# Two of the four weight sums of a Strassen pair moved to GpSimd, and every product made seven blocks wide

## The chip, the cores and the metric

The kernel runs on one core of a Trainium2 chip. A core has a matrix engine (PE, with its weight loads shown apart as PEld), a vector engine (DVE), an activation engine (ACT), GpSimd (POOL), a queue engine (SP) and 16 DMA engines; on-chip data lie in SBUF, and matmul results in eight PSUM banks. The metric is the device time of one execution in microseconds (us). Before the change it is 2906.9 us, the median of three runs (2904.82 to 2906.92).

## The reference

One layer of a hybrid encoder on 512 tokens with model width 2048: an input projection, a gated-DeltaNet group and an RWKV-7 group, an output projection, cross-attention into 256 memory tokens, an MLP and a last norm, all in float32.

```python
def reference(x, mem, ...):
    h = x
    for l in range(DEPTH):                      # DEPTH = 1
        xn = _rmsnorm(h, norm_mix[l])
        y = xn @ w_in[l]
        ...
        h = h + mixed @ w_out[l]
        h = h + _cross_attention(...)
        hn = _rmsnorm(h, norm_mlp[l])
        h = h + jnp.square(jax.nn.relu(hn @ mlp_w_up[l])) @ mlp_w_down[l]
    return _rmsnorm(h, norm_final)
```

The change lies in `hn @ mlp_w_up`, a 512x2048 by 2048x8192 product, called Up here. The product with `mlp_w_down` after it is called Down.

## The kernel before

**Numbers.** Each float32 operand is cut into a high and a low part. ACT casts the 128x1024 weight block to the high part (`whi`), DVE subtracts that from the block and gets the low part (`wlo`). A cut is this pair, `cut` at L1771. A product is high times high, high times low and low times high. The activations `cb` hold both parts side by side, 256 columns of each. So for each of 8 inner blocks there is one matmul of `whi` on 512 columns and one of `wlo` on the 256 high columns, and the two halves of the PSUM bank are added when it is read.

**Strassen.** Up is made in 32 units. A unit is a pair of 128-row output blocks, and has four weight blocks of 128x1024: A11, A21, A22, A12. Seven products take the place of eight, in this order, each with its weight operand: B11 (A11), T1 (s1), T2 (s2), B21 (A12), T3 (s3), B22 (s4), T4 (A22). The four weight sums are made on the chip, one unit ahead or within the unit, by `adds` (L1839):

- s1 = A21 + A22 and s2 = s1 - A11, each in one of two buffers named `ws`
- s3 = A11 - A21, over A21's own buffer
- s4 = A12 - s2, over A12's own buffer, after A12 has been cut for B21

So the s1 of the next unit may only overwrite a `ws` buffer when the old s1 has been used, and the s2 of the next unit when s4 has read the old s2. The activation sums are made before Up.

**Banks.** B11, T2, T3 and T4 of a unit add up in one PSUM bank (`mx`), T1 and B22 in a second (`mg`), B21 has a third (`mm`). Between two products of one bank its contents are taken out: `grab` (L2004) by an ACT copy of one half and a DVE add of the other, `gains` (L2008) by DVE adds of both halves. PE must not start T2 before B11 has been grabbed, T3 not before T2, T4 not before T3's gains, and B22 not before T1's grab. A DVE add out of PSUM is 128x256 and stands in the trace as `sl` or `acc` from `mxu`, `mgu` or `mmu`.

**Narrow products.** In the even units B21 is narrow (`narrow`, L2012): the high weights are multiplied with each 256-column half by a matmul of its own, both into the same 256 columns of the bank. That makes 16 matmuls of 256 columns in place of 8 of 512, and one DVE add instead of two.

**Buffers.** There are three pairs of `whi` and `wlo`, so the cut for a product may begin when the product three places earlier is done with its part. Six buffers (`wraw` and `w`) hold weight blocks as they come from memory; a block's buffer is free after its last use.

**Beside it on DVE.** In the units 1 to 8, DVE makes four 128x256 differences of the preceding unit's outputs (`differences`, L2029). From unit 8 on, it also makes weight sums for Down (`presum`, L393) where the planner sees room: 128x512 sums in `ab`, 128x256 sums in `h`, each with loads and a store over SP's queue.

**The planner.** Generators such as `adds`, `splits`, `multiply_` and `upout` yield operations. `run` (L284) keeps a modelled clock for each engine and issues next the operation whose modelled start, plus a charge for its rank, comes first. The modelled prices are in `cost` (L210): a DVE 1024-wide sum is 154 + 1.05 ns a column, a POOL operation 235 + 2.3 ns a column. The result is one fixed order for each engine, and at run time an engine waits at the head of that order. All operations of Up stand at L256 in the profile, the line of the planner that issues them.

Of the kernel before, what the change touches and what calls it, by code (L numbers as in the profile page):

```python
# [12 lines left out]
ALU = mybir.AluOpType  # L13
# [60 lines left out]
def build(tc, I, out):  # L74
# [133 lines left out]
    DV, AC, GS, TE, SY = (Lane(e, k) for e, k in ((V, "DVE"), (S, "ACT"), (GP, "POOL"), (PE, "PE"), (nc.sync, "SP")))  # L208
# [72 lines left out]
    def after(*ev):  # L281
        return lambda: ev in events
# [103 lines left out]
    A11, A21, A22, A12 = range(4)  # L386
# [31 lines left out]
    raws, halves, used, whole, piece = {}, {}, set(), set(), {}  # L418
# [889 lines left out]
    B11, T1, T2, T3, T4, B22, B21 = range(7)  # L1308
# [448 lines left out]
    def take(lst):  # L1757
        yield lambda: bool(lst)
        return lst.pop(0)
# [8 lines left out]
    def tt(o, a, b, op=ALU.add):  # L1768
        return DV.tensor_tensor(out=o, in0=a, in1=b, op=op)
# [7 lines left out]
    raws, sums, halves = {}, {}, {}  # L1777
# [41 lines left out]
    def ready(*keys):  # L1819
        return lambda: all(("raw",) + k in events or ("sum",) + k in events for k in keys)  # L1820
# [12 lines left out]
    def release(u, i, lst=None):  # L1833

        left[u, i] = left.get((u, i), {A11: 3, A21: 2, A22: 2, "s1": 2, "s2": 2}[i]) - 1
        if left[u, i] == 0:
            (wfree if lst is None else lst).append(raws[u, i] if lst is None else sums[u, i])

    def adds():  # L1839
        for u in units:  # L1840
            if u[0] == "d":
                continue
            yield ready((u, A21), (u, A22))
            sums[u, "s1"] = s1 = yield from take(sfree)
            yield tt(s1, raws[u, A21], raws[u, A22])
            events.add(("sum", u, "s1"))
            release(u, A22)
            yield ready((u, A11))
            sums[u, "s2"] = s2 = yield from take(sfree)
            yield tt(s2, s1, raws[u, A11], ALU.subtract)  # L1850
            events.add(("sum", u, "s2"))
            release(u, A11)
            release(u, "s1", sfree)
            sums[u, "s3"] = a21 = raws[u, A21]
            yield tt(a21, raws[u, A11], a21, ALU.subtract)
            events.add(("sum", u, "s3"))
            release(u, A11)
            release(u, A21)
            yield ready((u, A12))
            yield after("cut", u, A12)  # L1860
            sums[u, "s4"] = a12 = raws[u, A12]
            yield tt(a12, a12, s2, ALU.subtract)
            events.add(("sum", u, "s4"))
            release(u, "s2", sfree)

# [64 lines left out]
    def multiply_():  # L1930
        for u in units:
# [38 lines left out]
            for i, w in order_of(u):  # L1970
                tag = {B21: "mm", T1: "mg", B22: "mg", T4: "scr" if first else "mx"}.get(i, "mx")
                if (u, tag) not in banks_of:
                    banks_of[u, tag] = yield from bank(tag, f"{tag}{kind}{e}_{g}")
                pt = banks_of[u, tag][0]
                fresh = i in (B11, B21, T1) or first and i == T4
                if not fresh:
                    yield after("snap", u, {T2: B11, T3: T2, T4: T3, B22: T1}[i])
                yield after("half", u, i)
                hi, lo = halves[u, i]
                for zs in (range(7), range(7, 8)) if first else (range(8),):  # L1980
                    for k in zs:
                        w_ = hi[:, k * P:k * P + P]
                        if narrow(e, i):
                            for part in (HA, HB):
                                yield mmr(pt[:, HA], w_, comb[i][k][:, part], fresh and k + part.start == 0)
                        else:
                            yield mmr(pt, w_, comb[i][k], fresh and k == 0)
                    for k in zs:
                        yield mmr(pt[:, HA], lo[:, k * P:k * P + P], comb[i][k][:, HA], stop=k == 7)
                if e == 31:  # L1990
                    tfree.extend(comb[i])
                hfree.append(halves[u, i])
                events.add(("mul", u, i))
                if i == B11:
                    chain(upout(u), 0.2)
# [14 lines left out]
            yield tt(o, o, pt[:, part])  # L2010

    def narrow(p, i):  # L2012
        return i == B21 and p % 2 == 0

    def squared_(p, j, c):
        yield AC.activation(c, c, AF.Relu)
# [28 lines left out]
    def upout(u):  # L2045
# [8 lines left out]
        if first:  # L2054
            yield mul(B21)
            y, ky = banks_of[u, "mm"]
            yield from gains(c1[:, HA], y, 2 - narrow(p, B21))
            events.add(ky)
# [22 lines left out]
        yield mul(B21)  # L2081
        y, ky = banks_of[u, "mm"]
        yield from gains(c1[:, HA], y, 2 - narrow(p, B21))
        events.add(ky)
        yield mul(T3)
# [209 lines left out]

    chain(loads(), 2)
    chain(adds(), 1.5)
    chain(insitu(), 1.5)
    chain(splits(), 1)
# [119 lines left out]
```

## Time and profile before

| what | value |
|---|---|
| median of three runs | 2906.9 us |
| the profiled execution, its time | 2904.46 us |
| its span | 2902.7 us |
| mean granted PE clock | 0.998 |
| PE busy | 2870.4 us, 99% of the span |
| DVE busy | 2330.4 us, 80% |
| ACT busy | 1570.0 us, 54% |
| POOL busy | 223.6 us, 8%, all of it in the first 1000 us |
| 128x1024 cut on DVE, mean in Up | 1221 ns |
| 128x1024 sum on DVE in Up, mean by buffers | 1215 to 1220 ns |

Up begins with the first matmul into `mxu` at 1644.3 us and ends near 2282 us; Down follows. Between 1650 and 2282 us PE is busy 630.3 us, DVE 567.5, ACT 358.6 and POOL not at all.

In a timeline row the first number is the start in us from the span's start, the second the duration, then engine, line, operation, output<-inputs, shapes, a count, and in brackets how long the engine was idle before it and what ended that. Rows of one DVE stream overlap a little: the next one's start is recorded before the last one's end.

### The profile page before, as it was taken

The page shows a single profiled execution, that of the slowest core. Times are in us where ns is not written, and L with a number is a line of the kernel's source. Part 1 is how long each engine was busy: PE and PEld are TensorE (multiplying, and loading weights), DVE is VectorE, ACT ScalarE, POOL GpSimd, SP SyncE. Part 2 cuts the span into 40 slices and gives each one's busy share as a digit, 9 for nine tenths or more (in the row PEclk, how much of TensorE's full clock was granted, in tenths as well). Part 3 has the DMA queues.
Part 4 walks back from the last instruction along what each step waited for, and adds up shares of the span by engine and source line. Part 5 has one row for each costly group of instructions (what it writes and reads, how often), then busy time and mean ns, then how long its engine had stood idle before and what let it go on. Part 6 is the DMA issues. An engine that isn't in the chain of part 4 may idle for free.

```text
span 2902.7 us, 49242 instructions
## 1 busy us (share of the span) xinstructions
PE 2870.4 (99%) x18794; PEld 2420.3 (83%) x18794; DVE 2330.4 (80%) x3547; ACT 1570.0 (54%) x2233; POOL 223.6 (8%) x547
## 2 busy tenths in 40 slices
PE   8999999999999999999999999999999999999998
PEld 7877877787877888889988888888888888888887
DVE  7787787787887877769956898898998878787888
ACT  6454555555655655564445656555555645454544
POOL 0213213213223000000000000000000000000000
PEclk9999999999999999999999999999999999999999
DMA  5646656656666788784423354565566868978733
GB/s 190 175 139 184 164 156 181 160 150 187 176 163 188 219 249 280 227 286 159 127 92 95 106 163 152 193 199 193 186 201 191 283 225 278 295 257 272 270 100 109
DMA packets 319773, 553.02 MB, mean 191 GB/s; under 512 B 100968, under 2 KB 186220, under 8 KB 319536
## 3 DMA queue, kind: packets, MB, share of 16 engines
q1 hardware_dynamic: 292144, 518.41, 58.0%
q10 hardware_dynamic: 27392, 31.46, 3.1%
q8 instruction: 147, 2.41, 0.3%
q14 instruction: 90, 0.74, 0.1%
HBM read 443.45 MB, written 106.31 MB: 189 GB/s over the span
## 4 chain that ended last, share of the span: by engine, by line
PE 93%; DMA 3%; DVE 2%; ACT 1%; issue 1%; POOL 0%; ACTq 0%; SPq 0%; DVEq 0%; POOLq 0%
PE py L256 22%; PE mxu L256 12%; PE mgu L256 6%; PE mgd L256 6%; PE mxd L256 6%; PE op L122 6%; PE vp L122 3%; PE sc L122 3%; PE at L122 3%; PE mmd L256 3%; PE kp L256 3%; PE mmu L256 3%; PE scrd L256 3%; PE scgd L256 3%; PE kq L256 3%; PE vo L122 1%
## 5 line engine op out<-in xcount | busy, mean ns | idle before, releaser
L256 ACT CAST whi<-wraw 128x1024 fp32r<-128x1024 f32 (+1 forms) x366 | 383.7, 1049 | 399.8 <-PE py L256 146.8
L256 DVE TENSOR_TENSOR wlo<-wraw,whi 128x1024 fp32r<-128x1024 f32 (+1 forms) x366 | 450.4, 1231 | 102.7 <-ACT whi L256 92.9
L256 PE MATMUL py<-xhi,whi 128*128 128x512 f32 x928 | 372.2, 401 | 7.8 <-ACT xhi L256 7.8
L256 PE MATMUL py<-xlo,whi 128*128 128x512 f32 x928 | 373.7, 403 | 0.0
L256 PE MATMUL py<-xhi,wlo 128*128 128x512 f32 x928 | 372.9, 402 | 0.0
L256 ACT CAST whi<-w 128x1024 fp32r<-128x1024 f32 x176 | 185.4, 1054 | 203.9 <-PE mxu L256 48.3
L256 DVE TENSOR_TENSOR wlo<-w,whi 128x1024 fp32r<-128x1024 f32 x176 | 214.8, 1221 | 51.5 <-ACT whi L256 49.5
L256 PE MATMUL mxu<-cb,whi 128*128 128x512 f32 x1016 | 255.0, 392 | 0.0
L256 PEld LDWEIGHTS py<-xhi,whi 128*128 128x128 f32 x928 | 175.0, 189 | 42.1 <-ACT xhi L256 7.8
L256 PEld LDWEIGHTS mxu<-cb,whi 128*128 128x128 f32 x1016 | 182.8, 189 | 32.7
L256 PEld LDWEIGHTS py<-xlo,whi 128*128 128x128 f32 x928 | 175.0, 189 | 35.5 <-DVE xlo L256 0.9
L256 PEld LDWEIGHTS py<-xhi,wlo 128*128 128x128 f32 x928 | 175.1, 189 | 35.1 <-issue 1.8
L131 DVE TENSOR_TENSOR wlo<-wraw,whi 128x1024 fp32r<-128x1024 f32 x112 | 136.6, 1221 | 45.5 <-ACT whi L130 42.5
L130 ACT CAST whi<-wraw 128x1024 fp32r<-128x1024 f32 x112 | 117.7, 1051 | 85.5 <-PE op L122 29.1
L256 PEld LDWEIGHTS mxu<-cb,wlo 128*128 128x128 f32 x1016 | 138.7, 190 | 10.5 <-DVE wlo L256 0.7
L256 PE MATMUL mxu<-cb,wlo 128*128 128x256 f32 x1016 | 142.2, 282 | 0.3 <-DVE wlo L256 0.3
L256 ACT ACT_TABLE_LOAD x87 | 111.6, 1283 | 36.4 <-DVE suml_gn L256 15.5
L256 PE MATMUL mgu<-cb,whi 128*128 128x512 f32 x512 | 129.4, 394 | 1.4 <-ACT whi L256 1.3
L256 PE MATMUL mxd<-whi,cb 128*128 128x512 f32 x512 | 126.7, 389 | 0.0
L256 PE MATMUL mgd<-whi,cb 128*128 128x512 f32 x512 | 126.5, 389 | 0.0
L256 ACT CAST whi<-ws 128x1024 fp32r<-128x1024 f32 x75 | 78.9, 1052 | 75.4 <-PE mgu L256 49.2
L122 PE MATMUL op<-ob,whi 128*128 128x256 f32 (+1 forms) x752 | 115.3, 304 | 0.0
(946 smaller groups left out, 6452.3 us busy)
## 6 DMA issues: line engine op xcount, KB each, us to landing
wraw<-in_w_in SPq DMA_DIRECT2D x116, 512.0 KB, 4.5
wraw<-in_w_up SPq DMA_DIRECT2D x65, 512.0 KB, 3.8
w<-in_w_up SPq DMA_DIRECT2D x63, 512.0 KB, 3.9
ds<-in_w_dm SPq DMA_DIRECT2D x128, 205.0 KB, 4.0
sd_s<-ds SPq DMA_DIRECT2D x128, 205.0 KB, 5.2
wraw<-sd_s SPq DMA_DIRECT2D x51, 512.0 KB, 5.1
w<-sd_s SPq DMA_DIRECT2D x50, 512.0 KB, 5.0
w<-in_w_dm SPq DMA_DIRECT2D x48, 512.0 KB, 5.1
```

The lines of the kernel that those rows point to most:

```text
L122: PE.matmul(o, l, r, start=start, stop=stop, skip_group_check=again)
L130: S.copy(hi, src)
L131: V.tensor_tensor(out=lo, in0=src, in1=hi.bitcast(F32), op=ALU.subtract)
L256: f(*a, **k)
```

## The change

In `adds`, s3 and s4 are issued on POOL (`GS`) instead of DVE. `narrow` returns False for all units, so B21 is 8 matmuls of 512 columns everywhere and its two halves are added by two DVE adds.

```diff
             sums[u, "s3"] = a21 = raws[u, A21]
-            yield tt(a21, raws[u, A11], a21, ALU.subtract)
+            yield GS.tensor_tensor(out=a21, in0=raws[u, A11], in1=a21, op=ALU.subtract)
             events.add(("sum", u, "s3"))
...
             sums[u, "s4"] = a12 = raws[u, A12]
-            yield tt(a12, a12, s2, ALU.subtract)
+            yield GS.tensor_tensor(out=a12, in0=a12, in1=s2, op=ALU.subtract)
...
     def narrow(p, i):
-        return i == B21 and p % 2 == 0
+        return False
```

64 sums of 128x1024 go from DVE to POOL, and 16 adds of 128x256 come to DVE. Since the planner sees other loads, the orders of Up change. Among the weight sums for Down, 71 of 128x512 stand on DVE within Up now and 47 before; of the 128x256 sums (with the differences) it is 64 and 46.

DVE, unit 13, from the cut of A12 to the adds out of `mm`, before. `wlo_262<-wraw271` is the cut of A12, `sl839<-mxu13` the grab of B11, `wraw271<-wraw271,ws1` is s4, `w22` holds s3, `acc2<-mgu13` is the grab of T1, `ws0` and `ws1` are written as s1 and s2 of unit 14.

```order
L256 TENSOR_TENSOR wlo_262_17948<-wraw271_17934,whi_262_17947 128x1024
L256 TENSOR_TENSOR sl839_17953<-mxu13_0_20234,sl839_17953 128x256
L256 TENSOR_TENSOR wraw271_17934<-wraw271_17934,ws1_17942 128x1024
L256 TENSOR_TENSOR wlo_263_17950<-w22_17939,whi_263_17949 128x1024
L256 TENSOR_TENSOR acc2_17155<-mgu13_0_20261,acc2_17155 128x256
L256 TENSOR_TENSOR ws0_17941<-w20_17937,w21_17938 128x1024
L256 TENSOR_TENSOR wlo_261_17946<-wraw271_17934,whi_261_17945 128x1024
L256 TENSOR_TENSOR sl839_17953<-mxu13_0_20234,sl839_17953 128x256
L256 TENSOR_TENSOR ws1_17942<-ws0_17941,wraw272_17935 128x1024
L256 TENSOR_TENSOR sl839_17953<-sl839_17953,mmu13_0_20312 128x256 x2
```

The second `sl839<-mxu13` is the grab of T2; here it stands ahead of the next unit's s2. The same place in the changed kernel:

```order
L256 TENSOR_TENSOR wlo_262_17948<-wraw271_17934,whi_262_17947 128x1024
L256 TENSOR_TENSOR sl839_17953<-mxu13_0_20223,sl839_17953 128x256
L256 TENSOR_TENSOR ws0_17941<-w20_17937,w21_17938 128x1024
L256 TENSOR_TENSOR wlo_263_17950<-w22_17939,whi_263_17949 128x1024
L256 TENSOR_TENSOR acc2_17155<-mgu13_0_20251,acc2_17155 128x256
L256 TENSOR_TENSOR ws1_17942<-ws0_17941,wraw272_17935 128x1024
L256 TENSOR_TENSOR wlo_261_17946<-wraw271_17934,whi_261_17945 128x1024
L256 TENSOR_TENSOR sl839_17953<-mxu13_0_20223,sl839_17953 128x256
L256 TENSOR_TENSOR ab1_17944<-ab0_17943,ab1_17944 128x512
L256 TENSOR_TENSOR sl839_17953<-sl839_17953,mmu13_0_20307 128x256 x2
```

s4 is gone from DVE, and both sums of unit 14 stand ahead of the grab of T2. All units from 10 to 30 have this order up to that grab. In units 1 to 8 the four differences stand between s1 and the grab of T1, the cut of s3 after that grab, and the cut of s4 after the grab of T2.

POOL, the whole of it in units 13 to 15 (s3 of 13, s4 of 13, s3 of 14 and so on). POOL has nothing else in Up, and had nothing there before.

```order
L256 TENSOR_TENSOR w22_17939<-w21_17938,w22_17939 128x1024
L256 TENSOR_TENSOR wraw271_17934<-wraw271_17934,ws1_17942 128x1024
L256 TENSOR_TENSOR w20_17937<-wraw272_17935,w20_17937 128x1024
L256 TENSOR_TENSOR w22_17939<-w22_17939,ws1_17942 128x1024
L256 TENSOR_TENSOR wraw273_17936<-wraw271_17934,wraw273_17936 128x1024
```

The s4 of a unit is followed directly by the s3 of the next.

PE, B21 of unit 0 (`mmu`), the difference between the two kernels at the high weights; lines with a minus stand before:

```order
-L256 MATMUL mmu_0_17990<-cb_2_17200,whi_17947 128x256 x2
-L256 MATMUL mmu_0_17990<-cb_3_17201,whi_17947 128x256 x2
-L256 MATMUL mmu_0_17990<-cb_4_17202,whi_17947 128x256 x2
-L256 MATMUL mmu_0_17990<-cb_5_17203,whi_17947 128x256 x2
-L256 MATMUL mmu_0_17990<-cb_6_17204,whi_17947 128x256 x2
+L256 MATMUL mmu_0_17990<-cb_0_17198,whi_17947 128x512
+L256 MATMUL mmu_0_17990<-cb_1_17199,whi_17947 128x512
+L256 MATMUL mmu_0_17990<-cb_2_17200,whi_17947 128x512
+L256 MATMUL mmu_0_17990<-cb_3_17201,whi_17947 128x512
+L256 MATMUL mmu_0_17990<-cb_4_17202,whi_17947 128x512
```

Two matmuls of 256 columns on one block of high weights become one of 512.

## The prediction

> **What bounds the kernel now.** I read the page's busy times and its chain of waits first, then a windows table of Up and of Down, then the timeline of one pair in Up.
>
> ```profile
> PE 2870.4 (99%) x18794; PEld 2420.3 (83%) x18794; DVE 2330.4 (80%) x3547; ACT 1570.0 (54%) x2233; POOL 223.6 (8%) x547
> ...
> PE 93%; DMA 3%; DVE 2%; ACT 1%; issue 1%; POOL 0%; ACTq 0%; SPq 0%; DVEq 0%; POOLq 0%
> ```
>
> ```profile
> 1650.00:2282.00 632.00, 630.31 (x3746) 559.83 (x3746) 567.50 (x754) 358.60 (x501) 0.00 (x0) 1.00 0.57 183
> 2300.00:2800.00 500.00, 500.00 (x2207) 414.02 (x2206) 400.29 (x477) 246.88 (x286) 0.00 (x0) 1.00 0.78 256
> ```
>
> The columns are stretch, length, busy us of PE, PEld, DVE, ACT and POOL, granted clock, DMA share, GB/s. In Up (first row) PE idles 1.7 of 632 us and DVE is busy 90%; in Down PE never idles. So taking work from DVE can save at most those 1.7 us in Up, and nothing in Down. A gain must shorten PE's own work; a loss comes from anything that makes PE wait. The next rows show how near PE is to waiting. It is pair 13; start and duration stand first.
>
> ```profile
> 1908.33 2.00 PE L256 MATMUL mxu<-cb,whi 128*128 128x512 f32 x8
> ...
> 1910.37 1.05 ACT L256 CAST whi<-wraw 128x1024 fp32r<-128x1024 f32 x1 [0.89 <-PE mxu L256]
> ...
> 1911.12 2.00 PE L256 MATMUL mgu<-cb,whi 128*128 128x512 f32 x8
> ...
> 1911.45 1.22 DVE L256 TENSOR_TENSOR wlo<-wraw,whi 128x1024 fp32r<-128x1024 f32 x1 [0.84 <-ACT whi L256]
> ...
> 1912.60 0.42 DVE L256 TENSOR_TENSOR sl<-mxu,sl 128x256 f32<-128x256 f32 x1
> ...
> 1912.93 1.22 DVE L256 TENSOR_TENSOR wraw<-wraw,ws 128x1024 f32<-128x1024 f32 x1
> ...
> 1913.91 2.00 PE L256 MATMUL mxu<-cb,whi 128*128 128x512 f32 x8
> ...
> 1916.71 2.00 PE L256 MATMUL mmu<-cb,whi 128*128 128x512 f32 x8
> ...
> 1918.19 0.42 DVE L256 TENSOR_TENSOR sl<-mxu,sl 128x256 f32<-128x256 f32 x1
> ...
> 1919.50 2.00 PE L256 MATMUL mxu<-cb,whi 128*128 128x512 f32 x8
> ```
>
> The PE rows are the starts of B11, T1, T2, B21 and T3: 2.79 us a product. The cut at 1911.45 waits for its cast, which waits for PE to be done with the high part of B11. The add at 1912.60 takes B11 out of its bank, that at 1918.19 takes T2 out. T3 accumulates in T2's bank, so it cannot start before that second add is done: 1918.61 against 1919.50, 0.89 us in hand. This is the wait that the change can bring about, once in each pair.
>
> **The price of two engines at once.** No 128x1024 sum on POOL is in this trace; the nearest is gEs, 128x512, from the mixer stage.
>
> ```profile
> 236.74 1.22 DVE L256 TENSOR_TENSOR wlo<-wraw,whi 128x1024 fp32r<-128x1024 f32 x1 [3.46 <-ACT whi L256]
> ...
> 345.77 0.21 POOL L256 TENSOR_TENSOR sr<-sr,sr 64x15 f32<-64x15 f32 x1
> ...
> 346.26 0.63 ACT L256 ACTIVATE gE<-gE 128x512 f32<-128x512 f32 x1
> ...
> 346.40 1.36 DVE L256 TENSOR_TENSOR wlo<-wraw,whi 128x1024 fp32r<-128x1024 f32 x1 [1.39 <-ACT whi L256]
> ...
> 346.97 1.94 POOL L256 TENSOR_TENSOR gEs<-gE,cst 128x512 f32<-128x512 f32 x1 [0.30 <-ACT gE L256]
> ...
> 348.10 1.37 DVE L256 TENSOR_TENSOR suml_gn<-sg,sumh_gn 128x512 fp32r<-128x512 f32 x1 [0.34 <-ACT sumh_gn L256]
> ...
> 569.74 1.31 POOL L256 TENSOR_TENSOR gEs<-gE,cst 128x512 f32<-128x512 f32 x1
> 569.76 2.37 DVE L256 TENSOR_TENSOR wlo<-wraw,whi 128x1024 fp32r<-128x1024 f32 x1 [1.73 <-ACT whi L256]
> ...
> 572.05 0.68 DVE L256 TENSOR_TENSOR suml_gn<-sg,sumh_gn 128x512 fp32r<-128x512 f32 x1
> ...
> 798.00 0.69 DVE L256 TENSOR_TENSOR y<-py,rstd 128x512 f32<-128x512 f32 x1 [1.52 <-PE py L256]
> 798.08 1.30 POOL L256 TENSOR_TENSOR gEs<-gE,cst 128x512 f32<-128x512 f32 x1
> ```
>
> The cut takes 1.22 us alone and 2.37 beside gEs: it ends 1.08 us after gEs, as if it had begun at 570.91, 0.14 before gEs ends. At 346.97 it is POOL that waits: 1.94 instead of 1.30, because a cut ran until 347.76; and the next DVE operation, 0.68 alone, takes 1.37. So a DVE operation with both inputs in SBUF and a POOL sum exclude each other, whole operation by whole operation. The row at 798.00, one input from PSUM (py), is 0.69 beside gEs, and gEs is 1.30: no exclusion there. POOL starts 0.08 us after its releaser (346.89 to 346.97).
>
> [...]
>
> A 128x1024 sum on POOL: from 15 to 512 columns the time grows from 0.21 to 1.30, 2.2 ns a column, so 1.30+512x2.2 ns = 2.40 us. Bounds: not under the 1.30 of half the size, not over twice 1.31, 2.62; I take 2.40 since the slope is the rows' own. Between two such DVE operations gEs cost 1.03 us, from 347.76 to 348.79 (348.10+1.37-0.68); with 1.10 more, 2.13.
>
> [...]
>
> **The change, part by part.** (1) Wide B21 in 16 pairs.
>
> ```profile
> 1936.26 2.08 PE L256 MATMUL mmu<-cb,whi 128*128 128x256 f32 x16
> ...
> 1939.14 2.00 PE L256 MATMUL mxu<-cb,whi 128*128 128x512 f32 x8
> ```
>
> The narrow B21 lasts 2.88 us, the wide one 2.79 (1916.71 to 1919.50). PE gains 16x0.09 = 1.4 us. DVE gets 16 more adds.
>
> (2) Sums off DVE.
>
> ```profile
> 1923.29 1.22 DVE L256 TENSOR_TENSOR wlo<-wraw,whi 128x1024 fp32r<-128x1024 f32 x1
> 1924.42 1.22 DVE L256 TENSOR_TENSOR w<-wraw,w 128x1024 f32<-128x1024 f32 x1
> ```
>
> Back to back, a 1024-wide operation holds DVE for 1.13 us (0.09 of each row overlaps the next) and a PSUM add for 0.33 (1912.60 to 1912.93). DVE loses 64x1.13 = 72 us, which by itself is worth nothing, since PE covers it.
>
> (3) The moved order and the new waits. I set 0 at T1's start (1911.12) and follow pairs 9 to 30 in the new order: the A12 cut, the B11 add, s1 of the next pair, the s3 cut, the T1 add, s2 of the next pair, the s4 cut, the T2 add. The first cut keeps its anchor in PE's release: 0.33 to 1.55 as in the row; the B11 add is at 1.48. s4 on POOL needs that cut and starts at 1.63, to 4.03. The next s1 would start at 1.81; it must wait to 3.89 (0.14 before POOL's end) and holds DVE to 5.02. The s3 cut goes to 6.15 (row end 6.24). POOL's next s3, ready since s1 ended at 5.11, waits for that cut and takes the place after it. The T1 add, from PSUM, passes (to 6.48). s2 of the next pair is stuck: it writes the buffer that s4 read, and is behind s3: 6.24+2.13 = 8.37, to 9.50. The s4 cut goes to 10.63, the T2 add ends at 11.05, and T3 starts 0.08 later at 11.13. Before, it started at 8.38 (1919.50). **PE stalls 2.75 us a pair.** T2's start (2.79) is safe: the B11 add is done at 1.90.
>
> In pairs 1 to 8 four 128x256 differences, both inputs in SBUF, stand between s1 and the T1 add, and the s3 cut behind that add. The first runs from 5.02 (row end 5.44), POOL's s3 gets in behind it, the other three go on from 7.57 to 8.56, the T1 add to 8.89, s3 cut and s2 to 11.15, the T2 add ends at 11.57, T3 starts at 11.65: 3.27.
>
> (4) The second half of the pair has to be covered by the four products after T3's start, 11.16 us. DVE has there four cuts (4.5 us), seven PSUM adds with the new one (2.3) and, in pairs 9 to 24, up to four 512-wide and two 256-wide sums for Down.
>
> ```profile
> L256 DVE TENSOR_TENSOR ab<-ab,ab 128x512 f32<-128x512 f32 x30 | 20.5, 684 | 0.0
> ...
> L256 DVE TENSOR_TENSOR h<-h 128x256 f32<-128x256 f32 x14 | 5.8, 416 | 0.0
> ```
>
> At 0.60 and 0.33 after the overlap these are 3.1 us, together 9.9. Some of the adds wait for PE; followed in their order, the last of these operations ends about 1 us before the next pair's first cut is released. So it fits, barely, and costs nothing; if not, the third rival. The planner puts 24 more of the 512-wide and 18 more of the 256-wide into Up, with their loads and stores on SP's queue and the weight loads behind them. A longer pair and a DMA share of 0.57 cover these. Down has fewer, but PE is full there: no gain.
>
> Pair 31 has no following s3; with its s4 alone the T2 add ends near 7.4, inside 8.38: nothing. Pair 0 I count as nothing.
>
> **Sum.** 22x2.75 + 8x3.27 - 1.4 = 60.5 + 26.2 - 1.4 = +85.3 us. The profiled execution took 2904.5 us, 1.8 beyond its span; the median of the runs, 2906.9, is 0.08% above it. So 2990 for such an execution and 2992 for the median. With POOL's sum at 2.62 it is 30x0.44 = 13 more; at the floor of 1.30, 30x2.2 = 66 less.
>
> **Rivals.** *They share after all* (other side): POOL and DVE overlap in Up without cost. Then s2 waits for s4 alone (4.40 to 5.53), the s4 cut for its cast, the T2 add ends near 7.3, before 8.38: no stall, 2905.5. In my sum DVE waits 2.08 for s4 and 1.89 for s3, 3.97 together; PE is spared when that sum is under 3.97-2.75 = 1.2 us. Against it: the 512-wide gEs alone cost 1.1. [...] That the change then still gains nothing, since narrow products cost only 0.09 us, is the same 2905.5.
>
> *Half the wait*: DVE gets in between POOL's operations sooner than gEs shows, say 2.0 instead of 3.97. Stall 0.8, 30x0.8 = 24: 2930.
>
> *DVE late in the second half too*: if that half overruns by 2 us, 1 us is left after its margin, 16x1 more, and with POOL's sum at 2.62, 13 more: 3021. For it: four sums for Down between PSUM adds that PE times.
>
> *Faster* needs more than the 1.4 and the 1.7 us PE has to give.
>
> **Chances.** Both sums block as computed: 0.75. Half the wait 0.10, late second half 0.08, sharing 0.05, something that makes it faster 0.02. A change under 0.2%, 5.8 us, can hardly be told from none. Faster 0.02, same 0.05, slower 0.93. The likeliest is 2992. The range goes down to 2945, into the half wait and the shorter POOL sum, and up to 3025, past the late second half.
>
> **What would show it.** In the profile after: POOL sums of 2.4 us alone and longer when a cut runs; s1, s2 and differences on DVE with means well over 1.22; PE idle before T3 (mxu) ended by the DVE add out of mxu, 2 to 3 us a pair; a pair of about 22.3 us instead of 19.5; B21 alike in all pairs at 2.79; Down unchanged. I am wrong if the DVE rows stay at 1.22 beside POOL, if PE waits for cuts instead of the T2 add, or if POOL's s3 regularly comes behind s2.

## The result and the profile after

The changed kernel takes 3024.1 us (median of four runs, 3021.9 to 3026.9) where the kernel before takes 2905.9 beside it: a ratio of 1.0413, 95% interval 1.0398 to 1.0427. That is 118 us slower. The prediction was 2992, 85 us slower: the direction and the place are right, the loss came out at 118 us instead of 85, with the time at the very upper edge of the range (3025). Put on the 2906.9 us that the prediction started from, the ratio gives 3027, just past that edge.

The page of the profiled execution (span 3021.1 us), busy times and chain of waits (the shares of the chain come to 44% here, so nothing is read from it):

```profile
PE 2916.2 (97%) x18666; PEld 2443.6 (81%) x18666; DVE 2389.1 (79%) x3507; ACT 1570.9 (52%) x2233; POOL 401.1 (13%) x611
...
PE 31%; DVE 9%; issue 2%; ACT 1%; DMA 1%; ACTq 0%; DVEq 0%; SPq 0%
```

PE has 128 matmuls less than before and is yet busy 46 us longer. That is the first sign that something other than waiting was added. The windows of Up and of Down (columns as in the prediction):

```profile
1642.00:2400.00 758.00, 681.29 (x3660) 588.70 (x3659) 650.02 (x755) 361.29 (x507) 175.30 (x64) 0.94 0.57 177
2400.00:2900.00 500.00, 499.30 (x2204) 413.07 (x2203) 378.37 (x446) 252.98 (x295) 0.00 (x0) 1.00 0.69 232
```

Up grew from about 638 to 758 us. Two things show there: PE is idle for 77 us, and the granted clock is 0.94, where it was 1.00. Down is as before. What PE waits for in Up (the waits of PE between 1650 and 2400 us: total, times, longest):

```profile
PE mxu L256 <- DVE sl L256: 71.9, 30, 2.6
PE scru L256 <- DVE cb L1313: 2.3, 1, 2.3
```

30 waits for the T2 add, one in each of the pairs 1 to 30, are nearly all of it. Pair 13 of the changed kernel, as the prediction set it out; T1 starts at 1952.48, which is its time 0:

```profile
1952.48 2.00 PE L256 MATMUL mgu<-cb,whi 128*128 128x512 f32 x8
...
1952.81 1.23 DVE L256 TENSOR_TENSOR wlo<-wraw,whi 128x1024 fp32r<-128x1024 f32 x1
...
1954.11 2.42 POOL L256 TENSOR_TENSOR wraw<-wraw,ws 128x1024 f32<-128x1024 f32 x1 [17.09 <-DMA ab<-in_w_dm]
...
1954.28 3.33 DVE L256 TENSOR_TENSOR ws<-w,w 128x1024 f32<-128x1024 f32 x1
...
1957.53 1.21 DVE L256 TENSOR_TENSOR wlo<-w,whi 128x1024 fp32r<-128x1024 f32 x1
1957.69 3.31 POOL L256 TENSOR_TENSOR w<-wraw,w 128x1024 f32<-128x1024 f32 x1 [1.16 <-DVE ws L256]
...
1958.67 0.41 DVE L256 TENSOR_TENSOR acc<-mgu,acc 128x256 f32<-128x256 f32 x1
...
1959.00 3.08 DVE L256 TENSOR_TENSOR ws<-ws,wraw 128x1024 f32<-128x1024 f32 x1
...
1962.01 1.21 DVE L256 TENSOR_TENSOR wlo<-wraw,whi 128x1024 fp32r<-128x1024 f32 x1
1963.14 0.41 DVE L256 TENSOR_TENSOR sl<-mxu,sl 128x256 f32<-128x256 f32 x1
...
1963.61 3.38 PE L256 MATMUL mxu<-cb,whi 128*128 128x512 f32 x8 [2.59 <-DVE sl L256]
1966.79 1.45 PE L256 MATMUL mxu<-cb,wlo 128*128 128x256 f32 x8
```

In order: the A12 cut, s4 on POOL, s1 of the next pair shut out by it (3.33 instead of 1.22), the s3 cut, POOL's s3, which waits for that cut (3.31 instead of 2.41), the T1 add out of PSUM, which nothing holds up (0.41), s2 of the next pair shut out by s3 (3.08), the s4 cut, the T2 add, and T3. T3 starts at 11.13, as predicted to the hundredth, after 2.59 us without work for PE. Start to start that is 2.75 us more than before, since neighbouring products overlap by 0.16.

The last two rows hold what the prediction lacks: T3's high part takes 3.38 us instead of 2.00. The next windows show the clock. The first two stretches are from pair 2, the next two from pair 3, the last two from pair 13; each is 3.413 us long.

```profile
1701.28:1704.69 3.41, 1.09 (x9) 0.89 (x7) 3.38 (x6) 2.19 (x3) 0.00 (x0) 1.00 0.51 154
1704.69:1708.10 3.41, 3.25 (x8) 2.58 (x9) 3.12 (x5) 0.08 (x1) 0.00 (x0) 0.50 0.81 241
1725.17:1728.58 3.41, 1.86 (x13) 1.50 (x11) 3.38 (x6) 1.48 (x3) 0.18 (x1) 1.00 0.26 91
1728.58:1732.00 3.42, 2.58 (x14) 2.25 (x15) 3.39 (x6) 1.17 (x2) 0.00 (x0) 1.00 0.85 242
```

```profile
1960.69:1964.10 3.41, 0.82 (x5) 0.57 (x4) 3.41 (x5) 0.46 (x1) 0.31 (x1) 1.00 0.32 123
1964.10:1967.51 3.41, 3.41 (x12) 2.74 (x11) 2.54 (x5) 0.49 (x1) 0.00 (x0) 0.50 0.97 246
```

In pairs 2 and 13 a stretch in which PE is busy for only 1.09 and 0.82 us is followed by one at half clock. In pair 3 the wait is as long as in pair 2 (2.4 us), but the boundary between two stretches falls into it: PE is busy 1.86 us in the one and 2.58 in the other, and the clock stays full. Up has 25 such half-clock stretches (the first from 1653.49, the last from 2370.29), all at whole multiples of 3.413 us from each other: one in pair 0, one each in pairs 2, 4, 6 and 8, and one in each of the pairs 11 to 30. In those 24 pairs (pair 0 aside), T3 takes 4.4 to 4.5 us instead of 2.79. In the other six pairs that waited it takes 2.90; these 0.11 us are called its restart in the table.

So the 118 us divide as follows. The parts are summed over the PE rows of pairs 0 to 31, start to start.

| part | predicted | measured |
|---|---|---|
| T3 late, pairs 11 to 30 | 55.0 | 55.1 |
| T3 late, pairs 9 and 10 | 5.5 | 3.5 |
| T3 late, pairs 1 to 8 | 26.2 | 18.2 |
| T3 at half clock, and its restart | 0 | 40.1 |
| pair 0 | 0 | 5.3 |
| wide B21 | -1.4 | -1.4 |
| sum | 85.3 | 120.8 |

The span grew by 118.4; the rest is small differences elsewhere (Up starts 2.2 us earlier, and a wait of 1.6 us in pair 31 is gone). The prediction's error is smaller than the missing 45 us of T3's slowness and pair 0, because it made the waits in the pairs 1 to 10 some 10 us too long. That is luck.

### The profile page after: what moved, and what is told of

It is laid out like the page before. It is cut to its first block, busy times and chain, and to the rows that moved or that the text cites. A ratio compares the mean times of both kernels' runs of the same rounds, so it can differ in the third digit from the quotient of the medians.

```text
span 3021.1 us, 49132 instructions
## 1 busy us (share of the span) xinstructions
PE 2916.2 (97%) x18666; PEld 2443.6 (81%) x18666; DVE 2389.1 (79%) x3507; ACT 1570.9 (52%) x2233; POOL 401.1 (13%) x611
## 5 line engine op out<-in xcount | busy, mean ns | idle before, releaser
L256 PE MATMUL mxu<-cb,whi 128*128 128x512 f32 x1016 | 293.4, 437 | 72.7 <-DVE sl L256 71.9
L256 PEld LDWEIGHTS mxu<-cb,whi 128*128 128x128 f32 x1016 | 205.7, 212 | 118.9 <-DVE sl L256 78.0
L256 DVE TENSOR_TENSOR wlo<-ws,whi 128x1024 fp32r<-128x1024 f32 x75 | 91.6, 1222 | 36.8 <-ACT whi L256 36.8
```

The source lines that it names most:

```text
L256: f(*a, **k)
```

## The experiments

All ratios are against the kernel before, run beside it on the same chip. Edits are shown against the changed kernel. The theory is the prediction's, that POOL's sums shut DVE out and make the T2 add late; the half clock was added to it after the result was seen.

**Each part alone.** First, wide B21 everywhere and all sums on DVE:

```diff
-            yield GS.tensor_tensor(out=a21, in0=raws[u, A11], in1=a21, op=ALU.subtract)
+            yield tt(a21, raws[u, A11], a21, ALU.subtract)
...
-            yield GS.tensor_tensor(out=a12, in0=a12, in1=s2, op=ALU.subtract)
+            yield tt(a12, a12, s2, ALU.subtract)
```

> All products wide, all four sums on DVE as before. Theory (a narrow B21 costs PE 0.09 us and nothing else): 16x0.09 = 1.4 us less, about 2904.5 us, not told from before. Rival (DVE at 90% in Up cannot bear 16 more adds of 0.33 us and the order that the planner makes with them): slower by more than 5.8 us, with PE waiting for DVE adds in the even pairs.

Measured 2903.3 us, ratio 1.0003 (0.9993 to 1.0012). Second, the sums on POOL and B21 narrow in even pairs as before (`narrow` returns `i == B21 and p % 2 == 0`):

> s3 and s4 on POOL, B21 narrow in even pairs as before. Theory (T3's start is set by the late T2 add, so B21's length lies inside the stall): the time of the changed kernel, 3024 +-4 us, so the whole loss comes with the sums. Rival (the two parts add up): 1.4 us above the changed kernel if narrow costs what it did; and if the wide products had a share in the loss, clearly below 3020.

Measured 3019.6 us, ratio 1.0401 (1.0386 to 1.0417), with PE's waits for the T2 add at 69.7 us in 30 waits. So the loss is from the sums: the 0.0012 by which this ratio is under that of the changed kernel lies within the two intervals.

**One sum at a time.** s3 alone on POOL (s4 back on DVE), then s4 alone (s3 back):

> Only s3 on POOL, s4 back on DVE, all products wide. The planner then puts the T2 add ahead of the next pair's s2. Theory (two POOL sums ahead of the T2 add make the stall; POOL's s3 here shuts out a cut that stands behind the add or just beside it): T2 add done near 6.4 to 7.0 us after T1's start, before 8.38, no stall, 2905 +-4 us, granted clock 1.00 in Up. Rival (each POOL sum costs its share): half of the loss, about 2965 us.

> Only s4 on POOL, s3 back on DVE, all products wide. The order has s2 of the next pair ahead of the T2 add, as in the changed kernel, but POOL brings one sum there, not two. Theory: s1 waits for s4 to 3.89 us after T1's start, s2 is done at 7.61 with nothing more to wait for; the T2 add ends at 8.03 in even pairs (no stall) and at 9.16 behind a cut in odd ones (stall 0.86 us, 11 pairs): about 10 us more, 2916 us, between 2906 and 2925, no half clock. Rival (order alone, no exclusion): no stall, 2905. Rival (each sum its share): about 2965.

s3 alone: 2917.5 us, 1.0046 (1.0030 to 1.0063), some 12 us over what was expected. The timeline of DVE, POOL and PE in one of its pairs:

```profile
2005.25 2.11 PE L256 MATMUL mxu<-cb,whi 128*128 128x512 f32 x8 [0.29 <-DVE sl L256]
...
2009.01 2.41 POOL L256 TENSOR_TENSOR wraw<-wraw,wraw 128x1024 f32<-128x1024 f32 x1 [16.61 <-DVE ws L256]
2009.18 3.33 DVE L256 TENSOR_TENSOR wlo<-w,whi 128x1024 fp32r<-128x1024 f32 x1
```

Here s3 falls behind the T2 add, which is in time, and hits a cut instead (3.33). No single deadline is missed by much, but DVE loses 2.1 us once a pair and then runs behind: in odd pairs T2 comes up to 0.5 us late, because it waits for the B11 add, in some even pairs T3 up to 0.8. The pairs 9 to 30 lose 9.6 us by it, and pair 0 another 3.1. What was overlooked is that DVE has no reserve of 2 us a pair.

s4 alone: 2917.6 us, 1.0050 (1.0035 to 1.0065), as expected. In the odd pairs from 11 on, and in pair 30, T3 is late by 0.9 to 1.0 us, start to start, in the even pairs from 10 to 28 not at all. T3 of pair 15:

```profile
1965.11 2.11 PE L256 MATMUL mxu<-cb,whi 128*128 128x512 f32 x8 [0.80 <-DVE sl L256]
```

In neither is there a stretch at half clock in Up, and the two losses of 14 us add up to 29, not 118: both sums together put two exclusions and the next pair's s2 ahead of one add, and that makes the wait long enough (2.59 us in pair 13) to bring the clock down.

**The order without the reading.** In the same places POOL now fills the buffers by three memsets, which take about as long as a sum (2.55 us), followed by the sum of 16 columns alone. The rest of s3 and s4 is not computed. The order on PE, ACT and DVE is that of the changed kernel.

```diff
-            yield GS.tensor_tensor(out=a12, in0=a12, in1=s2, op=ALU.subtract)
+            yield [GS.memset(a12[:, part], 0.37) for part in (slice(0, 1024), slice(0, 1024), slice(0, 512))] + [
+                GS.tensor_tensor(out=a12[:, 0:16], in0=a12[:, 0:16], in1=s2[:, 0:16], op=ALU.subtract)]
```

> The changed kernel with the same order on PE, DVE and ACT, but on POOL each of the 64 sums is three memsets of 1024, 1024 and 512 columns and a sum of the first 16 columns alone (s3 and s4 are not made beyond these; the waits on both operands stay). POOL is busy about as long, 2.5 us, but hardly reads SBUF. Theory (DVE operations with two SBUF inputs wait only for POOL operations that read SBUF): s1 and s2 keep 1.22 us, the T2 add ends near 7.2 us after T1's start, before 8.38: no stall, 2905 +-5 us. Rival (the moved order and POOL's latency make the loss): 3015 to 3030 us.

Measured 2901.4 us, ratio 0.9992 (0.9983 to 1.0002): no loss at all. POOL and DVE in one pair:

```profile
1951.69 0.88 POOL L256 TENSOR_TENSOR w<-w,ws 128x16 f32<-128x16 f32 x1
1952.52 2.54 POOL L256 MEMSET w<- 128x1024 f32 x3
...
1952.74 1.21 DVE L256 TENSOR_TENSOR ws<-ws,w 128x1024 f32<-128x1024 f32 x1
1953.87 1.22 DVE L256 TENSOR_TENSOR wlo<-w,whi 128x1024 fp32r<-128x1024 f32 x1
```

s2 and a cut take 1.21 and 1.22 us beside the memsets, while the 16-column sum, 0.22 us alone, takes 0.88 beside a cut. So neither the new order nor the latency on POOL costs anything (ratio 0.9992); the loss needs POOL's sums themselves, which read SBUF, beside DVE operations with two inputs there. POOL's memsets, which only write, hold up neither s2 nor the cut.

**The clock by itself.** Ten matmuls of 512 columns into a bank that nothing reads, ahead of T3 in pairs 10 to 30, then four instead of ten. They do nothing but occupy PE while it waits.

```diff
+                if i == T3 and 10 <= e <= 30:
+                    if e == 10:
+                        idle.append(psb("idle", "scr", 1))
+                    for k in range(10):
+                        mm(idle[0], comb[B11][k % 7][:, 0:P], comb[T1][k % 7])
```

> The changed kernel, and in pairs 10 to 30 ten matmuls of 512 columns on PE ahead of T3, into a bank that nobody reads: 10x0.23 = 2.3 us of the 2.59 us in which PE waits. Theory (T3 is slow because PE's idle time brings a 3.41 us stretch at half the granted clock): the stalls stay, T3 goes from 4.4 back to 2.79 us in 20 pairs, 20x1.62 = 32 us less, about 2991 us, clock 1.00 in pairs 11 to 30. Rival (T3 is slow for another reason, as the cuts or the bank): 3024 or more.

> As the run with ten matmuls, with four: 0.9 us, so that 1.6 to 1.7 us of idle time are left a pair. In the changed kernel pairs 9 and 10 idled 1.62 and 1.54 us and kept the full clock, pairs 2 to 8 idled 2.38 us and lost it every second time. Theory (it is the length of the idle stretch): no half clock in pairs 11 to 30, about 2991 us. Rival (any regular stall brings it): 3015 to 3024.

Ten: 2992.1 us, 1.0304 (1.0288 to 1.0319). Four: 2993.2 us, 1.0306 (1.0291 to 1.0322). Windows that lie within the pairs 10 to 30, in the changed kernel and then with four fillers:

```profile
1900.00:2380.00 480.00, 428.18 (x2249) 369.43 (x2249) 407.17 (x466) 218.52 (x302) 114.50 (x40) 0.93 0.62 191
```

```profile
1890.00:2350.00 460.00, 425.79 (x2381) 366.65 (x2380) 417.09 (x479) 221.73 (x305) 115.03 (x41) 1.00 0.66 203
```

T3 starts as late as in the changed kernel, but takes 2.9 us, and the clock is 1.00: summed over the pairs, T3 takes 94.4 us with ten fillers instead of 126.6. The difference of 32 us is the time gained (3024.1 to 2992.1, or 1.0413 to 1.0304). With four fillers about 1.66 us of each wait is still idle, and that does not bring the clock down. The early pairs, which have no fillers, still have three half-clock stretches on T3 where the changed kernel has four.

**Another order, by prices.** If DVE were to make the T2 add before s1 and s2 of the next pair, PE should not wait. The planner sets the order by its prices, so a higher price of POOL might do it: 6.0 ns a column in place of 2.3 for all of POOL's operations, and then 4.6 for the 1024-wide ones alone.

```diff
-            return 116 + 0.75 * n if nm == "memset" else 235 + 2.3 * n
+            return 116 + 0.75 * n if nm == "memset" else 235 + (4.6 if n == 1024 else 2.3) * n
```

> The changed kernel with the planner's price of a POOL operation raised from 2.3 to 6.0 ns a column. The order of DVE then has the cut of A12, s1 of the next pair, the T1 add, the s3 cut, the T2 add and only then s2. POOL's s3 is ready when s4 ends. If DVE gets in between two POOL sums: the s3 cut runs from 5.8 us after T1's start, the T2 add ends near 7.3, before 8.38: no stall, 2905 to 2912 us. If POOL keeps its turn for a second sum that is ready: the s3 cut waits for both, the T2 add ends near 9.5, 1.1 us of stall in some 22 pairs, about 2930 us. Either way the granted clock stays at 1.00.

> The changed kernel with the planner's price of the 1024-wide POOL sums alone doubled (4.6 ns a column), so the stages ahead of Up keep their order. DVE then has the T2 add ahead of the next pair's s2 from pair 9 on, with one or two sums for Down between the T1 add and the T2 add; pairs 1 to 8 keep the order of the changed kernel. Theory (two POOL sums, each a whole operation long, still lie ahead of the T2 add): s1 ends at 5.02 us after T1's start, the s3 cut at 6.15, the sum for Down waits for s3 to 8.37 and the T2 add ends near 9.4: 1.1 us of stall in 22 pairs = 24, the 18 us of stalls in pairs 1 to 8 with four or five half-clock stretches (7) as in the changed kernel, and 5 for pair 0: 50 to 55 more than before, about 2955 us. Rival (the place of s2 ahead of the T2 add is the cause): stalls only in pairs 1 to 8, about 2930 us.

At 6.0: 2992.5 us, 1.0308 (1.0293 to 1.0324), far from what was expected. 31 us of it lie ahead of Up, which starts at 1675 us, because the price also reorders earlier stages; and Up still takes 692 us, 54 more than before. There PE waits for the T2 add 23 times, 35.4 us in all and up to 3.0 at once, and the expectation that the clock stays full failed too: T3 meets a half-clock stretch in the pairs 12, 15, 18 and 21. Its timeline shows who goes first when both engines wait:

```profile
1969.86 3.31 POOL L256 TENSOR_TENSOR wraw<-wraw,ws 128x1024 f32<-128x1024 f32 x1 [17.00 <-DVE wlo L256]
...
1971.24 3.02 DVE L256 TENSOR_TENSOR wlo<-w,whi 128x1024 fp32r<-128x1024 f32 x1
...
1973.14 3.40 POOL L256 TENSOR_TENSOR w<-wraw,w 128x1024 f32<-128x1024 f32 x1
...
1974.52 2.30 DVE L256 TENSOR_TENSOR h<-h 128x256 f32<-128x256 f32 x1
```

s4 ends at 1973.17. The cut that waits for it ends at 1974.26, so it went in 1.22 us earlier, at 1973.04, ahead of s3, which is next on POOL; s3 ends at 1976.54 and so went in at 1974.13, and the 256-wide sum behind the cut waits for s3 in its turn. The prediction let DVE in behind one POOL sum in the same way. It is not a rule, though. In the mixer stage of the kernel before, a cut waits behind POOL's COPY and is then passed by gEs:

```profile
681.26 0.62 POOL L256 COPY sr<-sr 64x256 f32<-64x256 f32 x1
681.49 2.73 DVE L256 TENSOR_TENSOR wlo<-wraw,whi 128x1024 fp32r<-128x1024 f32 x1 [1.98 <-ACT whi L256]
681.85 1.28 POOL L256 TENSOR_TENSOR gEs<-gE,cst 128x512 f32<-128x512 f32 x1
```

The cut ends at 684.22 and so went in at 683.00, after gEs.

At 4.6: 2961.2 us, 1.0194 (1.0177 to 1.0211), near the 2955 of the expectation. PE's waits for the T2 add are 37.2 us in 27 waits, 2.4 us each in the pairs 4 to 8 and about 1.1 from pair 10 on, and the clock stays full but for the pairs 0, 4, 6 and 8.

**Another order, by a planner that knows of the exclusion.** The planner gets one more clock: a POOL or DVE sum with two SBUF inputs starts in the model only when the last such one has ended.

```diff
-        return t
+        return max(t, clock["PORT"]) if port(op) else t
...
+            if port(op):
+                clock["PORT"] = t + d
```

> The changed kernel, with a planner that in Up holds one more clock: a DVE operation with two SBUF inputs and a POOL sum may not overlap. Its order puts s1 and s2 of a pair together ahead of the last add of the pair before, the T2 add directly behind the T1 add, and no sums for Down between the products of pairs 9 to 28. Theory (the loss is made by POOL sums ahead of an add with a deadline, not by the amount of work): stalls of less than 0.5 us a pair in Up, no half clock, 2905 to 2925 us, and never faster than before by more than 2 us since PE has no more to give. Rival (DVE and POOL together are too much for a pair of 19.5 us in any order: 9 x 1.13 + 10 x 0.33 + 2 x 2.2 = 17.9 us without sums for Down): still over 2940 us. If the sums for Down that leave Up come too late in Down, PE waits there instead.

Measured 3026.4 us, 1.0421 (1.0406 to 1.0437), as slow as the changed kernel. But the time is lost elsewhere. Windows of Up and of Down, and PE's waits in Down:

```profile
1645.00:2301.00 656.00, 642.73 (x3667) 563.22 (x3666) 533.34 (x658) 359.78 (x504) 181.51 (x64) 0.99 0.44 140
2301.00:3020.00 719.00, 617.85 (x2693) 508.37 (x2691) 538.69 (x658) 312.15 (x382) 0.00 (x0) 0.93 0.70 236
```

```profile
PE mxd L260 <- ACT whi L260: 72.1, 3, 43.5
PE scrd L260 <- ACT whi L260: 21.6, 2, 20.7
```

Up is 16 us longer than before, and that lies in the pairs 0, 1 and 5 (7, 6 and 5 us more), with half-clock stretches in pairs 1 and 5 that the expectation did not have; what these early pairs wait for was not taken apart. The pairs 10 to 30 take 19.55 us each, with no wait at all, though both sums are on POOL: the next pair's s1 and s2 stand together near the pair's end, just ahead of the T4 add. In return the planner puts hardly any sums for Down into Up (one `ab<-ab,ab`, where the kernel before has 30 and the changed one 48). They are made in Down, and PE waits there 94 us in five long waits, for casts of weights that come by way of those sums. The next kernel lets only 1024-wide operations exclude each other in the model:

```diff
-        return state.get("port") and op[0] in ("DVE", "POOL") and op[1] == "tensor_tensor" and len(two) > 1
+        return state.get("port") and op[0] in ("DVE", "POOL") and op[1] == "tensor_tensor" and len(two) > 1 and op[5].free_size() == 1024
```

> As the run before it, the planner's own clock now lets DVE and POOL exclude each other, but only for 128x1024 operations with two inputs in SBUF; the 512-wide sums for Down are planned as in the changed kernel. In the order that comes out, s1 and s2 of the next pair stand behind the T2 add and the B21 add, so that T3 no longer waits for them, and the sums for Down stand in Up again (62 of the 128x512 kind, 71 in the changed kernel, 47 before, 3 in the run before). My theory, that the loss in Up is s1 and s2 standing ahead of the T2 add while POOL shuts them out, and that the run before lost its 94 us only in Down, for sums that were made there: no stall before T3 from pair 10 on, 19.55 us a pair, Down at 620 us or little more, 2903 to 2925 in all (the early pairs may lose some 10 to 20 us, as in the run before). Rival, that two POOL sums a pair cost DVE too much in Up once it also has the sums for Down: pairs 10 to 28 of 20.5 us and more, PE waiting for cuts or adds, 2930 to 2990.

Measured 2947.4 us, 1.0148 (1.0131 to 1.0165). The theory's 2903 to 2925 is missed, and the rival's figure holds: with the sums for Down back in Up, Down is as short as before, and Up takes 679 us. Of the 41 us that this is above the kernel before, 20 lie in the pairs 0 to 8, as far as the theory allowed for, and 23 in the pairs 9 to 30, where it had none. Pair 13 on POOL, DVE and PE:

```profile
1939.96 2.41 POOL L260 TENSOR_TENSOR wraw<-wraw,ws 128x1024 f32<-128x1024 f32 x1 [12.87 <-DVE wlo L260]
...
1940.13 2.79 DVE L260 TENSOR_TENSOR ab<-ab,ab 128x512 f32<-128x512 f32 x1
...
1948.00 2.41 POOL L260 TENSOR_TENSOR w<-wraw,w 128x1024 f32<-128x1024 f32 x1 [5.63 <-DVE ws L260]
...
1948.62 2.87 DVE L260 TENSOR_TENSOR wlo<-wraw,whi 128x1024 fp32r<-128x1024 f32 x1
...
1953.56 2.07 PE L260 MATMUL mxu<-cb,whi 128*128 128x512 f32 x8 [0.85 <-DVE acc L260]
```

s4 now shuts out a sum for Down (2.79 instead of 0.68) and s3 a cut (2.87 instead of 1.22). That costs DVE 2.1 and 1.7 us, where making a 1024-wide sum itself costs it 1.13. So in the later pairs DVE falls behind, and PE waits 0.5 us before T3 (at 1946.84) and 0.85 before T4. Pairs 15, 21, 24, 27 and 30 take 19.55 to 19.57 us; in pair 15 s4 falls into 1.7 us in which DVE waits anyway. None of these orders is faster than the kernel before.

## Why the prediction was right and wrong

- *The exclusion and its price.* Right. In pair 13 s1 takes 3.33 us and s2 3.08 where 1.22 is their own time, POOL's sum takes 2.41 (2.40 was estimated from the 512-wide sum), and the T1 add out of PSUM is not held up (0.41). The groups of Up, POOL first:

```profile
L256 POOL TENSOR_TENSOR wraw<-wraw,ws 128x1024 f32<-128x1024 f32 x17 | 41.0, 2409 | 272.3 <-DVE wlo L256 202.1 <-DMA ab<-in_w_dm 51.2 <-DMA sd_s<-ab 17.1
L256 POOL TENSOR_TENSOR w<-w,w 128x1024 f32<-128x1024 f32 x11 | 34.4, 3127 | 14.7 <-DVE ws L256 14.7
```

```profile
L256 DVE TENSOR_TENSOR ws<-ws,w 128x1024 f32<-128x1024 f32 x16 | 41.9, 2620 | 0.0
...
L256 DVE TENSOR_TENSOR ws<-wraw,w 128x1024 f32<-128x1024 f32 x10 | 32.9, 3289 | 0.2 <-DVE sl L256 0.2
```

- *The price of POOL's sum.* The slope of the trace's own rows gave 2.40, 2.41 is measured.
- *T3 at 11.13, 2.75 us late.* Right for pairs 11 to 30, 2.75 on average, and right step by step in pair 13. For pairs 9 and 10 it was 1.7 to 1.8: the order assumed for them does not hold, since in both the T2 add stands ahead of the s4 cut. The order that the section on the change gives for units 10 to 30 holds from 11 on.
- *Pairs 1 to 8, 3.27 us each.* Too high: 2.5 to 2.6, and 0.3 in pair 1. Pair 3:

```profile
1717.96 1.23 DVE L256 TENSOR_TENSOR wlo<-w,whi 128x1024 fp32r<-128x1024 f32 x1 [0.42 <-ACT whi L256]
1718.41 2.08 PE L256 MATMUL mgu<-cb,whi 128*128 128x512 f32 x8
...
1723.01 2.62 DVE L256 TENSOR_TENSOR ab<-sl,sl 128x256 f32<-128x256 f32 x1
...
1729.42 2.11 PE L256 MATMUL mxu<-cb,whi 128*128 128x512 f32 x8 [2.38 <-DVE sl L256]
```

  The path is the predicted one (POOL's s3 gets in behind the first difference, and the second takes 2.62). But the A12 cut was taken to begin 0.33 us after T1, from pair 13. In these pairs transposes stand between B11 and T1, and the cut begins 0.45 us before T1. That is 0.78 us off each of the waits in pairs 2 to 8. Pair 1 has another order than was given for units 1 to 8: its differences stand ahead of the A12 cut and its s1 behind the s3 cut, so that s4 alone holds up DVE (a cut of 2.42 us) before the T2 add. In all it is 8 us.
- *The second half of the pair.* Right: it fits, T4 is not late. That rival had the time nearest to the result (3021), by a mechanism that did not happen.
- *Pair 0 counted as nothing.* 5.3 us: POOL's sums shut out the activation sums that pair 0 waits for (one of 128x256 at 1648.60 takes 2.33 us; `cb`, the wait of 2.3 at `scru`), and one stretch at half clock.
- *The term that was missing.* The sum priced PE's work after each wait at its old duration. The failed step is "PE stalls 2.75 us a pair", taken as the whole price of the wait; the sum has no term for a slower PE after it. In 24 of 30 pairs PE then runs a stretch of 3.413 us at half clock, 1.6 us more each, and with the restarts that is 40 us against nothing. For the pairs 11 to 30 the fillers show that it is the clock: 32 us come back with T3 starting as late as before. The trace of before could have warned only weakly, as it has one half-clock stretch amid its span, at 933 us, and no wait like these.

## What to carry to other kernels

Moving two-input sums from DVE to POOL bought nothing here, beside two-input DVE work: each of them still takes its turn, POOL's turn is twice as long (2.41 us against 1.22), and the sums removed from DVE come back as waiting (DVE is busy 2389.1 us with 64 sums less, 2330.4 before). Before such a move, look for the PSUM add that frees a bank for PE and count what stands ahead of it on DVE with two SBUF inputs. And price a wait of PE as the wait plus what the clock takes back: in Up, with up to 1.7 us idle in a stretch of 3.413 it was only the wait, with over 2 us it was 1.6 us more.

## What the runs showed of the hardware

- **The clock follows how much of a stretch is idle, not the length of one wait.** In the changed kernel every half-clock stretch from 923 us to 2370 us is 3.413 us long and lies on one fixed grid. The wait in pair 2 left PE idle for 2.32 us of one stretch, and half clock followed; that of pair 3 was split into 1.55 and 0.84 us of two stretches, and the clock stayed full. In Up of the changed kernel a full-clock stretch with 1.68 us idle or less was always followed by full clock and one with 2.26 or more always by half. With nine of the experiments set beside it, one with 1.76 us idle or less was always followed by full clock and one with 1.95 or more always by half; between, 1.79 and 1.88 were followed by half and 1.83 and 1.90 by full. So in Up of these runs the limit lay between 1.76 and 1.95 us of the 3.413. It is not sharp everywhere: ahead of Up, two stretches with only 1.50 and 1.59 us idle were followed by half (at 743 us with the POOL price of 6.0, at 933 us with s3 alone on POOL). Why was not tried.
- **The pairs lock to that grid.** A pair with the wait and a full clock takes 22.4 us (with fillers). With the half-clock stretch it takes 23.9 to 24.0, and seven stretches are 23.893 us: from pair 11 on the wait meets the same place of the grid each time, so every pair pays. In pairs 2 to 8 two pairs take 47.7 us, fourteen stretches are 47.8, and every second pair pays.
- **POOL's memsets, which only write, did not hold DVE up:** s2 took 1.21 us and a cut 1.22 beside them, against 3.08 for s2 beside a POOL sum.
- **Who goes first when both wait is open.** The cut at 1971.24 got in between two POOL operations, the one at 681.49 did not. What decides it was not tried.
